# The 32-row block inversion of a gated delta rule, moved from VectorE to GpSimd

## The chip, the cores and the metric

The kernel runs on one core of a Trainium2 chip. A core has five engines that run beside each other, each through its own instructions in order: TensorE (PE; matmuls and transposes), VectorE (DVE; elementwise work and reductions), ScalarE (ACT; elementwise functions and copies), GpSimd (POOL; elementwise work and DMA issue) and SyncE (SP; here the main issuer of DMAs). They wait for each other through semaphores. The metric is the time of one execution in device microseconds (us).

## The reference: what is computed

A two-layer decoder trunk on 512 tokens of 1024 features. The first layer mixes tokens with a gated delta rule (6 heads of width 128), the second with a sliding-window attention; each layer also attends to 256 memory tokens and ends in a SwiGLU block. All weights are f32. What matters here is the triangular system that the delta rule solves for each head and chunk:

```python
decay = jnp.exp(jnp.where(tril, gc[..., :, None] - gc[..., None, :], -jnp.inf))
kb = k * beta[..., None]
lower = jnp.where(strict, jnp.einsum("bhncd,bhnkd->bhnck", kb, k) * decay, 0.0)
rhs = jnp.concatenate([v * beta[..., None], kb * jnp.exp(gc)[..., None]], axis=-1)
sol = lax.linalg.triangular_solve(lower, rhs, left_side=True, lower=True, unit_diagonal=True)
u, w = sol[..., :dv], sol[..., dv:]
...
def step(state, inp):
    u_n, w_n, a_n, qg_n, kg_n, gl_n = inp
    v_new = u_n - jnp.einsum("bhck,bhkv->bhcv", w_n, state)
    o_n = jnp.einsum("bhck,bhkv->bhcv", qg_n, state) + jnp.einsum("bhcs,bhsv->bhcv", a_n, v_new)
    state = state * gl_n[..., None, None] + jnp.einsum("bhck,bhcv->bhkv", kg_n, v_new)
    return state, o_n
```

## The kernel before

Activations lie transposed, features on partitions and the 512 tokens along the row. Each f32 product is made of three matmuls on parts of reduced precision: ScalarE rounds a weight tile of 128x1024 to `whi` (L138), VectorE subtracts it from the raw weight to get `wlo` (L151, called from `split`, L166), and TensorE multiplies (`mm3`, L196). A weight tile passes through three stations: a DMA on SP into `wraw` (two buffers), `whi` and `wlo` (three buffers each), and 24 matmuls of 512 columns into a PSUM bank `pj`.

The delta rule works on chunks of 128 tokens, 24 of them (6 heads by 4 chunks). For each the inverse of a unit lower triangular 128x128 matrix is needed. `gdn` (L552) writes the 32x32 blocks on its diagonals to DRAM (`basein`), and `base_inverse` (L772) reads all 96 of them back as one tile `big`, a block in each partition (L780). There the inversion runs in 31 steps of two elementwise operations (L786 to L791): step j multiplies what is left of column j of L by row j of X into `btmp`, and subtracts that from the rows of X below. Every operation needs the result of the one before it; the shapes go from 31x1 over 16x16 to 1x31, so at most 256 elements in a partition. Then ScalarE makes a transposed copy of X (`big<-big`, L793), two DMAs store X and the copy to DRAM (`basex`, `basext`, L797) and eight load them back as blocks of `X64` and `Tt` (L804, L809). `solve` (L812) builds the 64- and 128-row inverses from these with small matmuls on TensorE, and `scan_step` uses them.

Beside the inversion run the scores and the softmax against the memory tokens (`scores`, L909; `sm` are its rows, scaled by VectorE and ScalarE in `scale`, L987), their transposes on TensorE into two PSUM banks `g` (L148), ScalarE's copies of these to `pf` (L1028), and the projections of the queries with their convolution (`qv`, L542; the first tap on ScalarE, three on VectorE) and gating.

The order on each engine is not the order of the code: a scheduler lays the instructions out when the program is built, by its own estimates of durations, with `nosync` ties (L114) where the author wants an order. On the chip each engine then keeps to its order, and an instruction that waits holds up all that stand behind it on its engine.

Of the kernel before, what the change touches and what calls it, by code (L numbers as in the profile page):

```python
# [13 lines left out]
ALU = mybir.AluOpType  # L14
# [70 lines left out]
class Builder:  # L85
# [686 lines left out]
    def base_inverse(self, gp, base_in, after):  # L772

        nc = self.nc
        n = NH * NB
        e = BASE * BASE
        whole = self.t(gp, [P, 4 * T], F32, "big")
        big = lambda i: whole[:n, i * e:(i + 1) * e].rearrange("p (a b) -> p a b", b=BASE)
        L = big(0)
        nc.sync.dma_start(L.rearrange("p a b -> p (a b)"), base_in.rearrange("n b e -> (n b) e"))  # L780
        X = big(1)
        Xf = X.rearrange("p a b -> p (a b)")
        clear = lambda out, value: self.nosync(nc.vector.memset(out, value).ins, after)
        clear(Xf, 0.0)
        clear(Xf[:, ::BASE + 1], 1.0)
        for j in range(BASE - 1):  # L786
            r, w = BASE - 1 - j, j + 1
            tmp = self.t(gp, [n, 256], F32, "btmp", 2)[:, :r * w].rearrange("p (i m) -> p i m", m=w)
            self.tt(nc.vector, tmp, L[:, j, j + 1:].unsqueeze(2).to_broadcast([n, r, w]),
                    X[:, j, :w].unsqueeze(1).to_broadcast([n, r, w]), ALU.mult)  # L790
            self.tt(nc.vector, X[:, j + 1:, :w], X[:, j + 1:, :w], tmp, ALU.subtract)  # L791
        Xt = big(0)
        self.copy(Xt, X.rearrange("p i m -> p m i"))  # L793
        outs = []
        for nm, src in (("basex", X), ("basext", Xt)):
            d = self.t(self.dpool, [NH, NB, BASE * BASE], F32, nm)
            nc.sync.dma_start(d.rearrange("n b e -> (n b) e"), src.rearrange("p a b -> p (a b)"))  # L797
            outs.append(d)
        X64 = self.t(gp, [P, NH, 2 * BASE], F32, "X64")
        clear(X64, 0.0)  # L800
        for b in range(NB):
            s = slice(b * BASE, (b + 1) * BASE)
            o = b % 2 * BASE
            nc.sync.dma_start(X64[s, :, o:o + BASE], outs[0][:, b, :].rearrange("n (i m) -> i n m", m=BASE))  # L804
        Tt = self.t(gp, [P, NH, P], F32, "Tt")
        clear(Tt, 0.0)
        for b in range(NB):
            s = slice(b * BASE, (b + 1) * BASE)
            nc.sync.dma_start(Tt[s, :, s], outs[1][:, b, :].rearrange("n (m i) -> m n i", i=BASE))  # L809
        return X64, Tt  # L810
# [916 lines left out]
```

## Time and profile before

| | us |
|---|---|
| three runs | 1116.79, 1117.61, 1118.80 (median 1117.61) |
| profiled execution, whole | 1117.12 |
| its span (first to last instruction) | 1115.4 |
| the inversion on VectorE, first start to last end | 110.98 to 148.61 |
| first use of its result on TensorE | 174.85 |

The profile lists, for one execution, the busy time of each engine, the chain of work that ended last, groups of equal instructions, and on request a timeline. A timeline row gives the start, the duration, the engine, the line, the operation with out<-in, and in brackets how long the engine had been idle and what ended that. "SPq" is SyncE's DMA queue. Matmuls are pipelined, so the starts of neighbouring ones tell more than their durations. The mean clock granted to TensorE was 0.999 of full speed.

### The profile page before, as it was taken

The page shows a single profiled execution, that of the slowest core. Times are in us where ns is not written, and L with a number is a line of the kernel's source. Part 1 is how long each engine was busy: PE and PEld are TensorE (multiplying, and loading weights), DVE is VectorE, ACT ScalarE, POOL GpSimd, SP SyncE. Part 2 cuts the span into 40 slices and gives each one's busy share as a digit, 9 for nine tenths or more (in the row PEclk, how much of TensorE's full clock was granted, in tenths as well). Part 3 has the DMA queues.
Part 4 walks back from the last instruction along what each step waited for, and adds up shares of the span by engine and source line. Part 5 has one row for each costly group of instructions (what it writes and reads, how often), then busy time and mean ns, then how long its engine had stood idle before and what let it go on. Part 6 is the DMA issues. An engine that isn't in the chain of part 4 may idle for free.

```text
span 1115.4 us, 21263 instructions
## 1 busy us (share of the span) xinstructions
PE 1103.7 (99%) x7957; PEld 1000.7 (90%) x7957; DVE 937.2 (84%) x1878; ACT 695.0 (62%) x1462; POOL 105.9 (9%) x129
## 2 busy tenths in 40 slices
PE   9999999999999999999999999999999999999997
PEld 8888778877889999999998777788899999999996
DVE  7676976667899999999997877839999899998964
ACT  8588674456566656665565655856766566655644
POOL 0000000000011111111110000000121111111101
PEclk9999999999999999999999999999999999999999
DMA  8344352234577777777753321115677877787622
GB/s 318 107 149 146 107 135 87 86 104 133 153 165 193 188 194 187 180 198 180 198 138 99 125 68 40 54 58 150 152 188 182 199 188 181 190 193 190 153 85 90
DMA packets 81146, 165.36 MB, mean 148 GB/s; under 512 B 18588, under 2 KB 20148, under 8 KB 81044
## 3 DMA queue, kind: packets, MB, share of 16 engines
q1 hardware_dynamic: 64436, 133.87, 38.1%
q0 software_dynamic: 16320, 29.89, 16.5%
q8 instruction: 62, 1.02, 0.4%
q14 instruction: 40, 0.33, 0.1%
q10 hardware_dynamic: 288, 0.26, 0.1%
HBM read 156.98 MB, written 7.01 MB: 147 GB/s over the span
## 4 chain that ended last, share of the span: by engine, by line
PE 84%; DVE 12%; ACT 2%; issue 1%; DMA 1%; DVEq 0%; ACTq 0%; SPq 0%
PE g L144 49%; PE pj L144 23%; PE sc L144 6%; DVE wlo L151 3%; PE qk L144 3%; PE pt L144 1%; DVE fu L151 1%; PE pt L148 1%; DVE x L151 1%; DVE l L154 1%; DVE T L151 1%; PE g L148 1%; DVE sqa L151 1%; DMA wraw<-in_wgu 1%; ACT h L138 1%
## 5 line engine op out<-in xcount | busy, mean ns | idle before, releaser
L138 ACT ACTIVATE whi<-wraw 128x512 fp32r<-128x512 f32 (+2 forms) x357 | 251.5, 712 | 154.9 <-PE g L144 70.1
L151 DVE TENSOR_TENSOR wlo<-wraw,whi 128x512 fp32r<-128x512 f32 (+2 forms) x357 | 280.6, 792 | 34.7 <-ACT whi L138 29.6
L144 PE MATMUL g<-T,whi 128*128 128x256 f32 x1280 | 229.2, 280 | 1.0 <-ACT fs L138 0.6
L144 PE MATMUL g<-h,whi 128*128 128x256 f32 (+1 forms) x780 | 222.5, 286 | 1.7 <-ACT h L138 1.5
L144 PE MATMUL g<-l,whi 128*128 128x256 f32 (+1 forms) x780 | 222.4, 285 | 0.0
L144 PE MATMUL g<-h,wlo 128*128 128x256 f32 (+1 forms) x780 | 222.1, 285 | 0.0
L144 PEld LDWEIGHTS g<-T,whi 128*128 128x128 f32 x1280 | 194.9, 188 | 2.1 <-ACT fs L138 1.1
L144 PE MATMUL pj<-h,whi 128*128 128x512 f32 (+1 forms) x460 | 182.1, 399 | 0.0
L144 PE MATMUL pj<-l,whi 128*128 128x512 f32 (+1 forms) x460 | 180.2, 392 | 0.4 <-DVE l L154 0.3
L144 PE MATMUL pj<-h,wlo 128*128 128x512 f32 (+1 forms) x460 | 179.7, 391 | 0.0
L144 PE MATMUL g<-T,wlo 128*128 128x256 f32 x640 | 178.4, 279 | 0.0
L144 PEld LDWEIGHTS g<-h,whi 128*128 128x128 f32 x780 | 146.3, 188 | 4.3 <-ACT h L138 2.5
L144 PEld LDWEIGHTS g<-l,whi 128*128 128x128 f32 x780 | 146.6, 188 | 1.8
L144 PEld LDWEIGHTS g<-h,wlo 128*128 128x128 f32 x780 | 146.6, 188 | 1.7
L144 PEld LDWEIGHTS g<-T,wlo 128*128 128x128 f32 x640 | 120.3, 188 | 0.0
L144 PEld LDWEIGHTS pj<-h,whi 128*128 128x128 f32 x460 | 86.3, 188 | 20.8 <-issue 4.1
L144 PEld LDWEIGHTS pj<-h,wlo 128*128 128x128 f32 x460 | 86.5, 188 | 18.0 <-issue 0.9
L144 PEld LDWEIGHTS pj<-l,whi 128*128 128x128 f32 x460 | 86.6, 188 | 17.6 <-DVE l L154 1.2
L138 ACT ACTIVATE whi<-ws 128x512 fp32r<-128x512 f32 x112 | 70.3, 628 | 47.0 <-PE g L144 45.6
L151 DVE TENSOR_TENSOR wlo<-ws,whi 128x512 fp32r<-128x512 f32 x112 | 76.9, 687 | 3.7 <-ACT whi L138 3.7
L1374 POOL DMA_DIRECT2D ws<-in_wgu x40 | 35.1, 878 | 438.2 <-DVE l L154 203.8
L138 ACT ACTIVATE fs<-g 128x256 f32<-128x256 f32 x168 | 61.2, 367 | 1.3 <-PE g L144 0.9
(398 smaller groups left out, 1927.2 us busy)
## 6 DMA issues: line engine op xcount, KB each, us to landing
wraw<-in_wgu SPq DMA_DIRECT2D x48, 512.0 KB
ws<-in_wgu SPq DMA_DIRECT2D x80, 256.0 KB
ws<-in_wgu POOLq DMA_DIRECT2D x80, 256.0 KB, 4.9
wraw<-in_win SPq DMA_DIRECT2D x26, 512.0 KB
wraw<-in_wgu SPq DMA_DIRECT2D x40, 256.0 KB
wraw<-in_wout SPq DMA_DIRECT2D x16, 512.0 KB
ws<-in_wdn SPq DMA_DIRECT2D x32, 256.0 KB
ws<-in_wdn POOLq DMA_DIRECT2D x32, 256.0 KB, 5.1
```

The lines of the kernel that those rows point to most:

```text
L138: self.copied = self.nc.scalar.activation(out, in_, AF.Copy, **kw).ins
L144: return self.nc.tensor.matmul(out, lhsT, rhs, start=start, stop=stop, skip_group_check=more).ins
L148: return self.nc.tensor.transpose(out, in_, self.ident[:k, :k]).ins
L151: return eng.tensor_tensor(out=out, in0=a, in1=b, op=op).ins
L154: return self.nc.vector.scalar_tensor_tensor(out=out, in0=in0, scalar=scalar, in1=in1, op0=op0, op1=op1).ins
L1374: nc.gpsimd.dma_start(s1, a22, accum_op=ALU.add)
```

## The change

The engine of the two operations in each of the 31 steps:

```diff
         for j in range(BASE - 1):
             r, w = BASE - 1 - j, j + 1
             tmp = self.t(gp, [n, 256], F32, "btmp", 2)[:, :r * w].rearrange("p (i m) -> p i m", m=w)
-            self.tt(nc.vector, tmp, L[:, j, j + 1:].unsqueeze(2).to_broadcast([n, r, w]),
+            self.tt(nc.gpsimd, tmp, L[:, j, j + 1:].unsqueeze(2).to_broadcast([n, r, w]),
                     X[:, j, :w].unsqueeze(1).to_broadcast([n, r, w]), ALU.mult)
-            self.tt(nc.vector, X[:, j + 1:, :w], X[:, j + 1:, :w], tmp, ALU.subtract)
+            self.tt(nc.gpsimd, X[:, j + 1:, :w], X[:, j + 1:, :w], tmp, ALU.subtract)
```

All shapes and data stay the same. The 62 instructions leave VectorE's list and stand on GpSimd's between the last of four early DMA issues (L484) and a memset (L1485), with the library load (`ISA`) that GpSimd's elementwise operations need ahead of them; before, that load stood ahead of four such operations at the end of the program. The scheduler also lays out the other engines anew around this place.

On ScalarE, behind the softmax of the first two memory heads (`sm_1275`, `sm_1276` are its rows, `qm_248` the second memory query, `big_1344` X and its transposed copy, `whi_1603` and `whi_1698` the rounded weights of two query projections):

```order
-L138 ACTIVATE sm_1275<-sm_1275,den_1278 128x256
+L138 ACTIVATE sm_1275<-sm_1275,den_1278 128x256 x2
 L138 ACTIVATE qm_248_1310<-pj_1318 128x512
-L138 ACTIVATE sm_1275<-sm_1275,den_1278 128x256
 L138 ACTIVATE sm_1276<-sm_1276,den_1278 128x256 x2
+L138 ACTIVATE big_1344<-big_1344 96x1024
 L138 ACTIVATE whi_1603<-wraw_1601 128x1024
 L138 ACTIVATE whi_1698<-wraw_1696 128x1024
```

The transposed copy of X has moved ahead of `whi_1603`; before, it stood sixteen rows behind that, after `whi_1828`. Behind `whi_1698` follow, before and now, the first tap of `qv_1590` and four copies `pf` of transposes. Also, `whi_1729` has moved back by some ten rows, behind the exponentials of the second softmax.

On SP, the loads of the query weights (`wraw`), the stores of the squared queries (`q<-sq`), and the way of the inverse through DRAM:

```order
 L177 DMA wraw_1696<-in_win 128x1024
-L177 DMA wraw_1727<-in_win 128x1024
-L177 DMA wraw_1826<-in_win 128x1024
-L695 DMA q_314_1647<-sq_1645 128x512
-L177 DMA wraw_2096<-in_win 128x1024
-L695 DMA q_317_1659<-sq_1657 128x512
 L797 DMA basex_1442<-big_1344 96x1024
 L797 DMA basext_1444<-big_1344 96x1024
 L804 DMA X_288_1446<-basex_1442 32x24x32 x4
 L809 DMA Tt_1452<-basext_1444 32x24x32 x4
+L695 DMA q_314_1647<-sq_1645 128x512
+L177 DMA wraw_1727<-in_win 128x1024
```

The stores and loads of the inverse now stand ahead of three weight loads and two stores that they used to follow; `wraw_2096` comes six rows further down, behind the store of the third squared query (`q_337`).

On TensorE the order at this place is the same before and now: projections of the queries (`pj_1519`) with the transposes of the softmax (`g`) and the products with the memory values (`sc_1527`) in between:

```order
 L148 MATMUL g_1531<-consts_66,sm_1275 128x128 x4
 L148 MATMUL g_1539<-consts_66,sm_1275 128x128 x4
 L144 MATMUL pj_1519<-h_506,whi_1515 128x512
 L148 MATMUL g_1552<-consts_66,sm_1276 128x128 x4
 L144 MATMUL sc_1527<-pf_1528,m_64_414 64x256 x2
```

Nothing moved here; the rows are those on which TensorE depends on ScalarE's `pf` copies. Further differences on TensorE and VectorE are shifts of neighbouring rows by a few places later in the same stage.

## Prediction

> **What bounds the kernel now.** I read the page first: shares, the tenths by slice, the chain that ended last.
>
> ```profile
> PE 1103.7 (99%) x7957; PEld 1000.7 (90%) x7957; DVE 937.2 (84%) x1878; ACT 695.0 (62%) x1462; POOL 105.9 (9%) x129
> PE 84%; DVE 12%; ACT 2%; issue 1%; DMA 1%; DVEq 0%; ACTq 0%; SPq 0%
> ```
>
> TensorE is the bound of the whole program: it carries 84% of the chain and is hardly ever without a matmul. A change elsewhere can win only where TensorE waits, and loses wherever it makes TensorE wait. GpSimd has next to nothing to do. The second view is busy time by stretch, over the time in which the inversion runs (columns: length; busy time and count of PE, PEld, DVE, ACT, POOL; granted clock).
>
> ```profile
> 111.00:127.70 16.70, 16.70 (x81) 13.40 (x80) 15.68 (x46) 11.57 (x27) 0.00 (x0) 1.00 0.35 116
> 132.60:148.60 16.00, 15.54 (x87) 11.67 (x86) 15.60 (x38) 7.63 (x12) 0.00 (x0) 1.00 0.28 97
> ```
>
> VectorE is full here (15.68 of 16.70, 15.60 of 16.00), which is what makes the move look attractive. But TensorE stands still for only 0.46 us of the later 16 us and for none of the earlier. Freeing VectorE can therefore give back about 0.5 us, not the time that VectorE is freed of.
>
> The third view is the timeline of VectorE and ScalarE at the two ends of the inversion.
>
> ```profile
> 110.98 0.19 DVE L151 TENSOR_TENSOR btmp<-big 96x31 f32<-96x31 f32 x1 [1.95 <-DMA big<-basein]
> 111.20 0.21 DVE L151 TENSOR_TENSOR big<-big,btmp 96x31 f32<-96x31 f32 x1
> ...
> 127.69 0.42 DVE L151 TENSOR_TENSOR btmp<-big 96x256 f32<-96x256 f32 x1
> ...
> 148.43 0.18 DVE L151 TENSOR_TENSOR big<-big,btmp 96x31 f32<-96x31 f32 x1
> ```
>
> ```profile
> 126.52 1.30 ACT L138 ACTIVATE sm<-sm,den 128x256 f32<-128x256 f32 x3
> 127.72 1.05 ACT L138 ACTIVATE whi<-wraw 128x1024 fp32r<-128x1024 f32 x1
> 129.95 1.06 ACT L138 ACTIVATE whi<-wraw 128x1024 fp32r<-128x1024 f32 x1 [1.18 <-PE pj L144]
> 130.91 0.67 ACT L138 ACTIVATE qv<-pj,gains 128x512 f32<-128x512 f32 x1
> 131.98 1.09 ACT L138 ACTIVATE pf<-g 128x512 f32<-128x512 f32 x2 [0.40 <-PE g L148]
> ...
> 148.70 2.00 ACT L138 ACTIVATE big<-big 96x1024 f32<-96x1024 f32 x1 [0.36 <-DVE big L151]
> 150.61 0.63 ACT L132 ACTIVATE qv<-qv 128x512 f32<-128x512 f32 x1
> ```
>
> The inversion starts when its input lands (110.98) and ends at 148.61. ScalarE's transposing copy of X (`big<-big`, L793) follows 0.09 us later and waited only 0.36 us, because it stands late in ScalarE's order. Its result is needed only by the solve's matmuls:
>
> ```profile
> 174.85 1.71 PE L144 MATMUL sc<-X,N 32*32 32x32 f32 x96
> ```
>
> So by the data there are 26 us of slack, and an inversion on a slower engine would be harmless **if nothing else stood behind it**. That is the question on which the forecast turns, and the instruction order answers it: in the changed program the copy stands ahead of `whi_1603`, right behind the scalings of `sm` that end at 127.82, where it used to stand sixteen rows later. ScalarE takes its instructions in order, so from 127.8 on it does nothing until GpSimd has finished.
>
> **The change, term by term.** Removed from VectorE: 62 operations (the window table, for the tile `btmp` alone).
>
> ```profile
> 111.00:148.70 37.70, 20.80 (x62) 1.00 0.31 105
> ```
>
> That is 20.80 us of work. Added to GpSimd: the same 62, with 2 x 5,456 = 10,912 elements in each partition (the sum of (31-j)(j+1) over j). Before has only four operations of this kind on GpSimd, and a few memsets:
>
> ```profile
> L151 POOL TENSOR_TENSOR T<-T,ws 128x256 f32<-128x256 f32 x4 | 2.8, 730 | 56.8 <-ACT ws L132 56.8
> L1485 POOL MEMSET sinT<- 128x512 f32 x1 | 0.5, 525 | 180.5 <-PE sc L144 180.5
> L283 POOL MEMSET ones<- 128x128 f32 x1 | 0.2, 204 | 0.3 <-POOLq L1718 0.3
> L1718 POOL MEMSET const-float32-0.0<- 128x1 f32 x1 | 0.1, 98 | 0.2 <-issue 0.2
> ```
>
> For 256 elements GpSimd takes 730 ns where VectorE takes 420 (127.69), a factor of 1.74. **Value taken:** 20.80 x 1.74 = 36.2 us. Bounds come from how the 730 ns divide. If the fixed part is only that of the smallest memset (98 ns), an element costs 2.47 ns and the 62 cost 6.1 + 26.9 = 33.0 us. If an element costs no more than in a memset ((525-204)/384 = 0.84 ns), the fixed part is 516 ns and they cost 32.0 + 9.1 = 41.1 us.
>
> Each of the 62 reads what the one before it wrote, so each also pays a hand-over. VectorE's is 0.03 us (110.98 + 0.19 to 111.20). The nearest row on GpSimd is its start behind ScalarE:
>
> ```profile
> 1104.01 0.38 ACT L132 ACTIVATE ws<-g 128x256 f32<-128x256 f32 x1
> ...
> 1104.47 1.43 POOL L151 TENSOR_TENSOR T<-T,ws 128x256 f32<-128x256 f32 x2 [53.65 <-ACT ws L132]
> ```
>
> It is 0.08 us, so 62 x 0.08 = 5.0 us; I take that, with 1.9 us (VectorE's gap) and 9.9 us (twice the row) as ends. The same row shows that the library load, an instruction that stood just ahead of this pair, cost nothing visible behind a long idle time. In the changed program it stands ahead of the inversion, where GpSimd has been idle since its last DMA issue (39.8 us), so it is taken at nothing.
>
> ```profile
> 38.69 1.07 POOL L484 DMA_DIRECT2D mk<-kt  x2 [4.34 <-DVE kt L151]
> ```
>
>
> GpSimd thus ends at 111.0 + 36.2 + 5.0 = **152.2 us**, with ends 145.9 and 162.0.
>
> What stands behind it: the copy starts at 152.2 + 0.09, `whi_1603` 1.91 later (148.70 to 150.61), then `whi_1698` and the `qv` scaling at 0.96 each (129.95 to 130.91) and, about 0.6 later, the first `pf` copy: 152.2 + 4.5 = 156.7, where it used to start at 131.98. The two waits of 1.18 and 0.40 in these rows are absorbed in that. **Delay 24.7 us**; in general the end of GpSimd's work minus 127.5.
>
> TensorE has nothing with which to cover it:
>
> ```profile
> 131.34 1.03 PE L148 MATMUL g<-consts,sm 128*128 128x128 f32 x8
> 132.13 0.47 PE L144 MATMUL pj<-h,whi 128*128 128x512 f32 x1
> 132.63 0.66 PE L148 MATMUL g<-consts,sm 128*128 128x128 f32 x4
> ```
>
> It makes eight transposes into the two `g` banks and one matmul; the next four transposes (132.63) need a `g` bank that only the `pf` copy frees, and every later matmul stands behind them. So TensorE stands still from about 132.4 to 157, and the delay goes through in full, since it is the bound from here to the end.
>
> **What is late next.** (a) After the pause TensorE may run slowly at first, as at the start of the program:
>
> ```profile
> 1.19 3.57 PE L144 MATMUL g<-wabs 128*128 128x256 f32 x15 [1.19 <-DVE eps L292]
> ...
> 6.62 0.29 PE L144 MATMUL pj<-mh,whi 128*128 128x256 f32 x1
> 6.74 0.28 PE L144 MATMUL pj<-ml,whi 128*128 128x256 f32 x1
> ```
>
> Fifteen matmuls of 256 columns took 0.24 us each there, and 0.12 from 6.62 on: some 5.4 us at half rate, 2.7 us lost. The granted clock of the page reads full throughout, so it doesn't decide what this was. I take 2 us, with ends 0 and 2.7. The Trainium skill ("TensorE: Matmul & The Clock Gate", section "What's actually happening") says that an idle window of about 3.4 us halves TensorE's clock until it has been busy for about as long. By that rule alone some 3.4 us at half rate would cost 1.7 us; without it the sum would be 2 us less.
>
> (b) On SP the two stores and eight loads of the inverse (148.63 to 156.38 in before) now stand ahead of three weight loads, and SP waits for GpSimd in front of them. The first two of those weights are wanted some 20 us after ScalarE resumes, and take cover behind `pj_1607` and `pj_1702`. The third, `wraw_2096`, now is issued behind the square of the third query, about 14 us later than before relative to TensorE's work:
>
> ```profile
> 143.05 0.33 SPq L177 DMA_DIRECT2D wraw<-in_win  x1
> ...
> 148.63 0.33 SPq L797 DMA_DIRECT2D basex<-big  x1
> ...
> 154.10 2.28 SPq L809 DMA_DIRECT2D Tt<-basext  x4
> ...
> ws<-in_wgu POOLq DMA_DIRECT2D x80, 256.0 KB, 4.9
> ```
>
> At 4.9 us or more for a landing (half its size took that), it comes about 2 us after ScalarE wants it, with two `pf` copies behind. I take 1 us, ends 0 and 3. (c) VectorE's freed time gives back the 0.5 us named above.
>
> Sum against the profiled execution (1117.12 us, 0.5 under the median of the runs shown): 24.7 + 2 + 1 - 0.5 = 27.2, so **1144.3 us**. Least: 145.9 - 127.5 - 0.5 = 17.9, or 1135. Most: 162.0 - 127.5 + 2.7 + 3 = 40.2, or 1157, and 1161 with the first rival.
>
> **The rivals.** *GpSimd and VectorE hinder each other.* Nothing in before shows it: GpSimd's four operations hardly differ (723 to 737 ns), and what VectorE ran beside them (`T<-T,g`) has one of its inputs in PSUM. VectorE still has two weight splits and four scalings before ScalarE stops:
>
> ```profile
> 114.03 1.21 DVE L151 TENSOR_TENSOR wlo<-wraw,whi 128x1024 fp32r<-128x1024 f32 x1
> ...
> 117.96 1.23 DVE L151 TENSOR_TENSOR wlo<-wraw,whi 128x1024 fp32r<-128x1024 f32 x1 [0.15 <-ACT whi L138]
> ...
> 124.74 0.34 DVE L994 TENSOR_SCALAR sm<-sm,den 128x256 f32<-128x256 f32 x1
> ...
> L151 POOL TENSOR_TENSOR T<-T,ws x4: 723/729/737, 1104.5 to 1109.7; 128x256 f32<-128x256 f32 x4
> ```
>
> If GpSimd stands still for all six it ends 3.8 us later: 1148. If VectorE's few operations wait instead, nothing changes. Chance 0.3, within the range. The Trainium skill ("SBUF — State Buffer", section "Who interferes with whom") has this as a lock on a shared port pair, held for a whole instruction; no run so far shows it.
>
> *The rows are too short for GpSimd.* The four known operations have rows of 128; the inversion's have 1 to 31, 992 rows in all. If a row costs as much again as its elements (36.2 / 992 = 0.036 us each), the inversion ends at 188 and the program at 1180. For it speaks nothing, against it nothing either. Chance 0.07.
>
> *Not slower: the wait never binds.* If GpSimd were done by 127.8, ScalarE's copy would find X ready. That needs 16.8 us for 62 operations, 0.27 us each, against 0.73 for the only size known; decisive point 0.27 us. Then the 0.5 us of TensorE's waits are won and the 2 us copy sits in idle time: 1116.6, no measurable change. The same if ScalarE could pass the copy by, which an in-order engine can't. A true gain would need more waiting on TensorE than the windows show. Chance 0.05, and 0.02 for a gain beyond 0.2%, about the least that a measurement of this kernel can tell from no change.
>
> **How the numbers follow.** Forecast (ScalarE blocked behind GpSimd, with or without the first rival): 0.86; short rows 0.07; not slower 0.07. The range 1132 to 1162 takes in the ends of the unknown costs and both forms of the forecast, and leaves out the short rows and the no-change case. Chances: faster 0.02, same 0.05, slower 0.93.
>
> **What would show it.** GpSimd's 62 operations should take 33 to 45 us from about 111, with 0.7 us for 256 elements and gaps under 0.16. ScalarE should show one wait of about 24 us in front of `big<-big`, released by GpSimd; TensorE a hole from about 132 to 157 that ends with a `pf` copy; behind it the same rows as before, shifted. Matmuls right behind the hole should be at half rate for a few us. I am wrong if ScalarE's wait is short, if GpSimd's operations take under 0.3 us, or if the rows at 175 stand where they stood.

## Result and the profile after

| | us |
|---|---|
| before, median of 4 runs beside the changed kernel | 1118.07 (1116.79 to 1118.80) |
| changed, median of 4 runs | 1143.63 (1141.50 to 1144.40) |
| ratio | 1.0227, 95% interval 1.0215 to 1.0239 |
| profiled execution of the changed kernel, whole / span | 1143.81 / 1142.0 |

The change costs 25.6 us. The page of the changed kernel, first part and two rows of the slices:

```profile
PE 1107.3 (97%) x7957; PEld 1003.6 (88%) x7957; DVE 921.3 (81%) x1816; ACT 695.4 (61%) x1462; POOL 138.5 (12%) x191
...
PE   9999659999999999999999999999999999999997
...
PEclk9999869999999999999999999999999999999999
```

TensorE does the same 7957 matmuls in about the same busy time (1107.3 us, 1103.7 before). Its share falls from 99% to 97% because of one hole, the 6 and the 5 in the fifth and sixth of 40 slices. The granted clock falls at the same place. VectorE is 15.9 us less busy (937.2 to 921.3), and that shows nowhere in the time.

The hole in the windows (columns: length; busy time and count of PE, PEld, DVE, ACT, POOL; granted clock), and the inversion alone on GpSimd (window table for the tile `btmp`):

```profile
132.60:157.00 24.40, 2.49 (x13) 1.53 (x13) 3.84 (x5) 5.37 (x6) 15.20 (x31) 0.58 0.22 49
155.10:160.10 5.00, 4.99 (x19) 3.33 (x20) 2.51 (x4) 1.93 (x4) 0.00 (x0) 0.50 0.84 133
```

```profile
111.50:150.20 38.70, 33.78 (x62) 0.82 0.15 50
```

Until GpSimd ends at 150.15, every other engine stands idle in the hole: the work of ScalarE (5.37 us) and VectorE (3.84 of 24.40 us) comes behind that. The timelines of ScalarE and TensorE name the waits:

```profile
127.91 0.90 ACT L138 ACTIVATE sm<-sm,den 128x256 f32<-128x256 f32 x2
150.18 1.94 ACT L138 ACTIVATE big<-big 96x1024 f32<-96x1024 f32 x1 [21.38 <-POOL big L151]
152.02 1.99 ACT L138 ACTIVATE whi<-wraw 128x1024 fp32r<-128x1024 f32 x2
153.91 0.67 ACT L138 ACTIVATE qv<-pj,gains 128x512 f32<-128x512 f32 x1
154.48 1.07 ACT L138 ACTIVATE pf<-g 128x512 f32<-128x512 f32 x2
```

```profile
132.73 0.47 PE L144 MATMUL pj<-h,whi 128*128 128x512 f32 x1
155.11 1.11 PE L148 MATMUL g<-consts,sm 128*128 128x128 f32 x4 [21.91 <-ACT pf L138]
156.16 1.98 PE L144 MATMUL sc<-pf,m 128*64 128x256 f32 x8
```

GpSimd's last subtraction ends at 150.15. ScalarE has waited 21.38 us for it with the copy of X, and TensorE 21.91 us for the `pf` copy that stands four instructions behind that copy. The eight products `sc<-pf,m` behind the hole take 1.98 us where they took 1.08.

How the loss builds up is read from equal rows of TensorE in both kernels, before first, then after:

```profile
136.75 0.50 PE L144 MATMUL pj<-h,wlo 128*128 128x512 f32 x1
150.88 0.59 PE L144 MATMUL sc<-m,qm 64*128 64x256 f32 x2
158.36 1.06 PE L144 MATMUL g<-qv,kn 128*128 128x128 f32 x8
```

```profile
161.59 0.50 PE L144 MATMUL pj<-h,wlo 128*128 128x512 f32 x1
174.66 0.59 PE L144 MATMUL sc<-m,qm 64*128 64x256 f32 x2
183.97 1.05 PE L144 MATMUL g<-qv,kn 128*128 128x128 f32 x8
200.48 1.71 PE L144 MATMUL sc<-X,N 32*32 32x32 f32 x96
```

The last matmul ahead of the hole already stands 0.60 us later than before (132.13 to 132.73). This is no work of the change: equal matmuls at 21 us, long before the inversion, are already 0.57 us apart. From there the shift grows to 22.48 at the transposes behind the hole (132.63 to 155.11), to 24.84 at 161.59, falls to 23.78 at 174.66, rises to 25.61 at 183.97 and is 25.63 at 200.48. So the terms are +21.88 (the wait), +2.36 (slow rows), -1.06 (small waits of before that are gone), +1.83 (a second place, at about 182). The sum is 25.0 us. The spans of the two executions differ by 26.6 us (1142.0 and 1115.4): besides these 25.0 and the 0.60 from the start, about 1.0 us more arises later than 200 us, most of it between 500 and 610 us, in work that the change doesn't touch. Its cause stays open.

### The profile page after: what moved, and what is told of

It is laid out like the page before. It is cut to its first block, busy times and chain, and to the rows that moved or that the text cites. A ratio compares the mean times of both kernels' runs of the same rounds, so it can differ in the third digit from the quotient of the medians.

```text
span 1142.0 us, 21267 instructions
## 1 busy us (share of the span) xinstructions
PE 1107.3 (97%) x7957; PEld 1003.6 (88%) x7957; DVE 921.3 (81%) x1816; ACT 695.4 (61%) x1462; POOL 138.5 (12%) x191
## 4 chain that ended last, share of the span: by engine, by line
PE 80%; DVE 9%; ACT 3%; POOL 3%; issue 2%; DMA 1%; SPq 0%; DVEq 0%; ACTq 0%; POOLq 0%
PE g L144 47%; PE pj L144 22%; PE sc L144 6%; DVE wlo L151 3%; PE qk L144 3%; POOL big L151 2%; POOL btmp L151 1%; PE pt L144 1%; DVE fu L151 1%; PE pt L148 1%; PE g L148 1%; ACT whi L138 1%; DVE x L151 1%; DVE T L151 1%; DVE l L154 1%
```

## Experiments

Two theories stood against each other. **Wait**: GpSimd's time costs nothing by itself, and what costs is that engines which take their work in order stand behind it. **Hindrance**: GpSimd's operations slow what runs beside them, or cost in some other way, whoever waits.

### The copy of X later (late_blocks, late_blocks_dve)

The function is cut in two, so that copy, stores and loads come after the next three query projections: the copy is tied behind ScalarE's work for the second memory head, the stores behind the load of the first value weight. The inversion stays where it was; late_blocks_dve is the same with the inversion on VectorE.

```diff
+            if h0:
+                first_v = self.load(a["win"][2 * H])
+                X, every_t = self.base_blocks(gp, *inverse, self.weighed_at, self.loaded)
...
-        Xt = big(0)
+        return X, big(0), clear
+
+    def base_blocks(self, gp, X, Xt, clear, copied, loaded):
...
         self.copy(Xt, X.rearrange("p i m -> p m i"))
+        self.nosync(self.copied, copied)
...
-            nc.sync.dma_start(d.rearrange("n b e -> (n b) e"), src.rearrange("p a b -> p (a b)"))
+            self.nosync(nc.sync.dma_start(d.rearrange("n b e -> (n b) e"), src.rearrange("p a b -> p (a b)")).ins, loaded)
```

> The inversion stays on GpSimd; ScalarE's transposing copy of X now stands behind mq1h (166 us in the trace of before), and SyncE's stores and loads of the inverse behind the load of the first value weight. Theory 'wait' (the 26.5 us are ScalarE standing in its order behind GpSimd, and TensorE behind ScalarE): no engine waits for GpSimd, so 1117 to 1119 us, as before the change, with TensorE's idle time before the transposes of sm under 1 us where it was 21.9. Theory 'hindrance' (GpSimd's operations slow VectorE and others beside them, whoever waits): 62 operations still run beside a busy VectorE, so at least a quarter of the loss stays: 1124 us or more. GpSimd's chain should get longer under both, since now VectorE works beside it: 38.6 us plus about 1.1 for each wlo that it meets.

> The same new places of the copy, the stores and the loads, with the 62 operations back on VectorE: the control for late_blocks. Theory 'wait': the places cost nothing, 1116 to 1119 us; and as the prediction gives the 20.8 us freed on VectorE only 0.5 us, late_blocks and this one lie within 1.5 us of each other. Rival ('VectorE binds here too'): the freed 20.8 us are worth more, and late_blocks is faster than this one by 2 us or more. Theory 'hindrance': this one is faster than late_blocks by 6 us or more.

Measured: late_blocks 1122.19 us, 1.0034 (1.0022 to 1.0046) of before; late_blocks_dve 1118.02 us, 1.0001 (0.9992 to 1.0010). Of 25.6 us some 4 stay, which is neither what wait said nor the 6 us that hindrance said. SyncE's queue, ScalarE and TensorE in late_blocks show where they go:

```profile
155.13 0.33 SPq L807 DMA_DIRECT2D basex<-big  x1
155.51 0.42 SPq L695 DMA_DIRECT2D q<-sq  x1
```

```profile
159.15 0.63 ACT L693 ACTIVATE sq<-qv 128x512 f32<-128x512 f32 x1 [3.24 <-DMA q<-sq]
```

```profile
163.47 1.73 PE L148 MATMUL g<-consts,sm 128*128 128x128 f32 x8 [3.13 <-DVE DT L151]
```

The store of X itself (`basex`) came out of the scheduler ahead of the store of a squared query. SyncE waited with it for GpSimd, the squared query lay behind it, and ScalarE waited 3.24 us for that query's only buffer. TensorE waited 3.13 us in turn, behind work of VectorE that depends on ScalarE, and the granted clock was 0.50 from 163.7 to 167.1. On SyncE, then, the same thing happens as on ScalarE.

### Both stores later too (late_stores, late_stores_dve)

```diff
-            nc.sync.dma_start(q2[h], sq)
+            self.q_stored = nc.sync.dma_start(q2[h], sq).ins
...
-                X, every_t = self.base_blocks(gp, *inverse, self.weighed_at, self.loaded)
+                X, every_t = self.base_blocks(gp, *inverse, self.weighed_at, self.q_stored)
```

> As late_blocks, with both stores of the inverse tied behind the store of the third squared query. In late_blocks the first of them (basex) stood on SyncE from 143 to 155 us for GpSimd, the store of a squared query behind it, and ScalarE's next square behind that for 3.24 us (its only buffer). Theory 'wait' (the 4.2 us of late_blocks are this third list that waits in order): 1117 to 1119 us, TensorE's busy time between 160 and 200 us back from 36.5 to over 39 us, and no wait of ScalarE for q. Theory 'hindrance' (GpSimd's operations cost it): 1121 us or more, as in late_blocks.

> The same places, with the inversion on VectorE: the control for late_stores. Theory 'wait' with the prediction's 0.5 us for a freed VectorE: within 1.5 us of late_stores. If VectorE's 20.8 us bind here: slower than late_stores by 2 us or more. If hindrance: faster than late_stores by 3 us or more.

Measured: late_stores 1118.12 us, 1.0003 (0.9994 to 1.0012); late_stores_dve 1118.57 us, 1.0010 (1.0001 to 1.0018). Against late_blocks, both stores of the inverse are now tied behind the store of the third squared query. A window of late_stores, then of late_stores_dve:

```profile
130.00:160.00 30.00, 29.98 (x163) 23.70 (x163) 20.74 (x36) 20.19 (x42) 20.41 (x33) 1.00 0.33 110
```

```profile
130.00:160.00 30.00, 29.55 (x157) 23.11 (x156) 26.72 (x63) 18.98 (x40) 0.00 (x0) 1.00 0.32 110
```

With all 62 operations still on GpSimd, beside a VectorE that works, nothing is lost: hindrance as a cause of the 25 us falls. GpSimd's chain even takes longer here (110.75 to 152.92, 42.2 us and not 38.6), since it meets more work of VectorE, and that costs nothing either. What the freed VectorE is worth shows only in TensorE's busy time, 29.98 of 30 us and not 29.55. The medians differ by 0.45 us the same way, but their intervals overlap, so a gain in time is not shown. The version on GpSimd without the waits is thus as fast as the kernel before; none of the versions tried beat it.

### The copy on GpSimd (copy_pool)

```diff
-        self.copy(Xt, X.rearrange("p i m -> p m i"))
+        nc.gpsimd.tensor_copy(Xt, X.rearrange("p i m -> p m i"))
```

> The transposing copy of X is done by GpSimd itself, behind its 62 operations; ScalarE's list loses this one instruction and keeps its order there, and SyncE's stores and loads of the inverse stay ahead of the weight loads that they passed. GpSimd ends at about 150.2 plus 2 to 3 us for the copy. Theory 'ScalarE is the one that holds TensorE': the 21.9 us before the transposes and the 2.4 us of slow clock behind them go; what stays is SyncE's list: wraw_1727 is issued at about 153 and not 139, its parts are ready at about 159 where TensorE needs them at 156, and two more weights follow behind eight loads: 3 to 8 us, so 1121 to 1126 us. Rival 'SyncE holds nothing that is needed': 1117 to 1119. Rival 'hindrance, or GpSimd is waited for elsewhere too': over 1130.

Measured: 1136.95 us, 1.0178 (1.0163 to 1.0192), far from the 1121 to 1126 expected and in the range of the last rival, of which the second half is true: GpSimd is waited for elsewhere too. SyncE, ScalarE and TensorE in this kernel:

```profile
154.22 0.38 SPq L177 DMA_DIRECT2D wraw<-in_win  x1
```

```profile
159.94 1.06 ACT L138 ACTIVATE whi<-wraw 128x1024 fp32r<-128x1024 f32 x1 [22.46 <-DMA wraw<-in_win]
```

```profile
165.25 2.08 PE L144 MATMUL g<-qv,kn 128*128 128x128 f32 x8 [18.92 <-ACT qv L132]
```

The wait of 21.9 us at the transposes is gone, as expected, but ScalarE stands for 22.46 us all the same. The load of `wraw_1727` is issued only behind the inverse's stores (`basext` at 153.80), and the scheduler, which does not know that, placed its rounding ahead of the next `qv`. I had reckoned with a late weight, not with what was queued behind it on ScalarE. With this order on ScalarE, SyncE's list costs 19.0 us without the copy of X: taking one engine out of the wait hands it to the next.

### The wait without GpSimd (early_dve)

The kernel before, inversion on VectorE, with one tie that puts ScalarE's copy of X ahead of a weight:

```diff
+            w = self.weight(a["win"][h0 + 2], after=() if h0 else (self.turned_x,))
+            ps += (self.project(None, self.h, w=w),)
...
+        self.turned_x = self.copied
```

> The kernel before, inversion on VectorE, with one tie: ScalarE rounds the third query weight behind the copy of X (it comes out behind the pf copies and the second qv). Nothing runs on GpSimd here that did not before. Theory 'wait': VectorE ends the inversion at about 148.6, ScalarE's copy takes 2.0 and the rounding 1.0, so the weight is there at about 151.7 where TensorE needs it at about 140: some 11 us, with 2.4 us of slow clock behind them and up to 2 us of later weights: 1128 to 1133 us with no work on GpSimd at all. Rival 'the loss needs GpSimd': 1117 to 1119 us.

Measured: 1128.22 us, 1.0093 (1.0079 to 1.0107), with nothing new on GpSimd. TensorE in this kernel:

```profile
146.42 0.50 PE L144 MATMUL pj<-h,whi 128*128 128x512 f32 x1 [4.42 <-ACT whi L138]
...
178.45 0.79 PE L144 MATMUL pj<-h,wlo 128*128 128x512 f32 x1 [1.62 <-DVE wlo L151]
```

The time is right, its parts are not: VectorE ended already at about 143.4, so the wait is 4.42 us and not 11; the rest is a wait of 0.86 us earlier, one of 1.62 us later, and two stretches at a lower clock, 0.50 from 146.9 to 150.4 and the second in this window:

```profile
177.66:184.48 6.82, 6.03 (x14) 4.77 (x15) 6.39 (x9) 2.21 (x3) 0.00 (x0) 0.50 0.47 124
```

That an order alone can make a loss of this kind is shown.

### More work on GpSimd, with and without the wait (double_mul, late_double)

In both, each multiplication is done twice. In double_mul a tie (that of early_dve) keeps the copy early on ScalarE; late_double is late_stores otherwise.

```diff
-            self.tt(nc.gpsimd, tmp, ...
+            for _ in range(2):
+                self.tt(nc.gpsimd, tmp, ...
```

> Each of the 31 multiplications is done twice (the second gives the same result), and the rounding of the third query weight is tied behind the copy of X so that the copy stays early on ScalarE; it comes out behind the first two pf copies instead of ahead of them. 31 multiplications more at 0.48 us (from the rows of the changed kernel, 15.0 us without the stretched one) and 0.077 us between two: GpSimd's chain 17.4 us longer, its end at about 167.6. Theory 'wait': the time follows GpSimd's end one to one, less what ScalarE now has done already (about 2): 1157 to 1161 us. Rival 'only a part of the loss is the wait, the rest a fixed price of the new order': well under one to one, 1150 us or less.

> late_stores with each of the 31 multiplications done twice. In late_stores GpSimd ended at 152.9 and the first instructions that need the result stood ready at 156.2 (SyncE, basex) and 165.5 us (ScalarE, the copy), TensorE's sc<-X,N at 173.9. 17.4 us more put GpSimd's end at about 170.3. Theory 'wait' (the operations cost nothing until the first list reaches a row that needs them, and then what is past the cover): stores, loads and copy come about 5 us later for ScalarE and X lands at about 176 to 178 where TensorE asks at 173.9; 2 to 6 us with the slow clock, 1120 to 1124 us. Rival 'GpSimd's time costs by itself': 1135 us, as 17 us more cost in double_mul. Rival 'still covered': 1118.

Measured: double_mul 1161.28 us, 1.0390 (1.0377 to 1.0404); late_double 1128.16 us, 1.0102 (1.0087 to 1.0117). ScalarE and TensorE in double_mul, then in late_double:

```profile
167.15 1.94 ACT L138 ACTIVATE big<-big 96x1024 f32<-96x1024 f32 x1 [33.06 <-POOL big L151]
```

```profile
170.10 1.97 PE L144 MATMUL sc<-pf,m 128*64 128x256 f32 x8 [33.67 <-ACT pf L138]
...
181.73 1.95 PE L144 MATMUL g<-qv,kn 128*128 128x128 f32 x16
196.81 0.80 PE L144 MATMUL pj<-h,whi 128*128 128x512 f32 x1 [4.26 <-ACT whi L138]
```

```profile
172.68 1.94 ACT L138 ACTIVATE big<-big 96x1024 f32<-96x1024 f32 x1 [7.40 <-POOL big L151]
```

```profile
179.81 2.08 PE L144 MATMUL g<-qv,kn 128*128 128x128 f32 x8 [7.03 <-ACT qv L132]
```

In double_mul GpSimd ends 17.0 us later than in the changed kernel (167.12 for 150.15), and the program takes 17.65 us more, just above the 1157 to 1161 expected. The totals agree one to one, the path does not. ScalarE got two `pf` copies and a `qv` done ahead of its wait, so TensorE's wait grew by 11.8 us only (33.67 for 21.91). A further 5.1 us were lost at a second place: from the sixteen products `g<-qv,kn` to the next ones (200.70) TensorE takes 18.97 us, and 13.85 in the changed kernel, because it waits 4.26 us for a weight that ScalarE rounds behind the second softmax, with a clock of 0.50 from 196.1 to 202.9. That the totals meet is luck; shown is that the wait grows when GpSimd ends later.

In late_double, GpSimd's end moved by 19.7 us (152.92 to 172.65) and the program by 10.0 (11 by the ratios to the kernel before, which ran beside each of the two). The first 12.6 us (from 152.9 to the copy at 165.47 in late_stores) were covered; past that ScalarE waits 7.40 and TensorE 7.03 us, with slow clock behind (0.50 from 179.8 to 189.4). The 2 to 6 us expected were too few: GpSimd ended 2.4 us later than reckoned, TensorE stood not for X but for a `qv` behind the copy, and the slow clock lasted longer.

### The slow rows behind the hole (warm, warm98)

Unused matmuls fill TensorE's wait:

```diff
+            if not own and m == 0 and n == 1:
+                hh = self.h[0][0]
+                for _ in range(90):
+                    ins = self.mm(o, hh[:, :P], hh)
+                    self.nosync(ins, turned)
+                    turned = ins
+                self.ahead = turned
```

> The changed kernel with 90 matmuls of 128x512 more, whose results nothing uses, on TensorE in the 22 us in which it waits (90 x 0.227 = 20.4 us). Theory 'the slow rows behind the wait come from the pause': the eight sc<-pf,m then take 1.08 us and not 1.98, and 2.4 us go: 1141 to 1141.8 us. Rival 'they come from something else that is late there (the copies, the loads)': the rows stay as long, 1143 to 1145 us.

> As warm, with 98 of the unused matmuls in place of 90. In warm the 90 ended at 152.9 and TensorE still waited 1.96 us; then the clock was 1.0 until about 155.6, 0.5 until about 158.4, and 1.0 again. 98 x 0.230 = 22.5 us end at 154.8, so no pause stays. Theory 'even a pause of 2 us brings the slow clock': the clock stays at 1.0, the eight sc<-pf,m take 1.08 us, and about 1.4 us (half of 2.8) go: 1139.3 to 1140.2 us. Rival 'the slow clock comes from something else at this place': 0.5 again for some us, 1141 us as in warm.

Measured: warm 1141.05 us, 1.0210 (1.0194 to 1.0226); warm98 1141.60 us, 1.0215 (1.0198 to 1.0232). TensorE in warm with windows behind its wait (columns: length, busy time and count of PE, granted clock, DMA share, GB/s), then in warm98:

```profile
154.88 1.50 PE L144 MATMUL sc<-pf,m 128*64 128x256 f32 x8 [1.96 <-ACT pf L138]
```

```profile
154.88:155.40 0.52, 0.52 (x6) 1.00 1.14 178
155.90:158.40 2.50, 2.50 (x13) 0.50 1.03 162
```

```profile
155.09 1.08 PE L144 MATMUL sc<-pf,m 128*64 128x256 f32 x8 [0.70 <-ACT pf L138]
...
159.58 1.08 PE L144 MATMUL sc<-pf,m 128*64 128x256 f32 x8 [1.46 <-ACT pf L138]
```

On the rows the theory holds. In warm98, with no long wait left, the clock is 1.00 from 153 to 160 and the products take 1.08 us. In warm a wait of 1.96 us was left, and the clock was 0.50 for 3.4 us (155.4 to 158.8). On the time the theory does not hold: warm98 is no faster than warm. At full clock TensorE waits for ScalarE instead (0.70 and 1.46 us), since the scheduler here placed a `qv` that waits for VectorE ahead of the second pair of `pf` copies. So the pause is shown to be the cause of the slow clock, while what the slow clock alone costs this program stays open: 2.36 us by the rows, less where ScalarE would have been late anyway. What warm gains in time may come from elsewhere: in its order `whi_1729` stands early again, which led to the next run.

### The second place (whi_first, after_again)

The changed kernel with the exponentials tied behind the rounding of `whi_1729`, and the changed kernel once more beside it:

```diff
-            steps = self.projected(a["win"][first + 1], self.h)
+            w = self.weight(a["win"][first + 1])
+            if m:
+                for e in self.exps:
+                    self.nosync(e, self.copied)
+            steps = self.projected(None, self.h, w=w)
...
+                        self.exps.append(self.fn(
```

> The changed kernel with the eight exponentials of the second softmax tied behind the rounding whi_1729, so that this weight stands on ScalarE where the kernel before had it, ahead of them. In the changed kernel it came at 180.46 and TensorE waited 0.67 us for it at 181.60 and 0.61 us for its wlo at 182.94; by its rows 1.83 us were lost there. Theory 'whi_1729 behind the exponentials is the last term': both waits gone, 1.2 to 1.9 us less than the changed kernel run beside it. Rival 'the softmax comes later in turn and TensorE waits for that': within 0.6 us of it.

> The changed kernel itself, on the same chip beside whi_first, as the measure for it: 1143 to 1144.5 us where the kernel before takes 1117 to 1118.5.

Measured: whi_first 1138.95 us, 1.0202 (1.0188 to 1.0216); after_again 1142.36 us, 1.0225 (1.0212 to 1.0239). TensorE in the changed kernel, then in whi_first:

```profile
170.12 1.95 PE L144 MATMUL g<-qv,kn 128*128 128x128 f32 x16
...
181.60 0.50 PE L144 MATMUL pj<-h,whi 128*128 128x512 f32 x1 [0.67 <-ACT whi L138]
182.94 0.50 PE L144 MATMUL pj<-h,wlo 128*128 128x512 f32 x1 [0.61 <-DVE wlo L151]
```

```profile
168.84 1.95 PE L144 MATMUL g<-qv,kn 128*128 128x128 f32 x16
180.82 1.06 PE L144 MATMUL g<-qv,kn 128*128 128x128 f32 x8
```

Both waits are gone. From the sixteen to the next eight products `g<-qv,kn` whi_first takes 11.98 us, the changed kernel 13.85 (170.12 to 183.97, shown above): 1.87 less, the term of 1.83. The medians differ by 3.4 us, more than the 1.2 to 1.9 expected of the tie. Some 1.1 us of the rest arose ahead of this place: GpSimd's chain ended 0.63 us earlier (149.15 for 149.78 in after_again), and the clock of 0.50 behind the hole lasted 4.5 us and not 5.5. The tie explains neither, and what is left stays open. after_again itself came out 0.6 us under the 1143 expected.

## Why the prediction was right, and where its sizes were off

The forecast was 1144.3 us, slower with a chance of 0.93; measured 1143.63. Point by point:

- **TensorE bounds; VectorE's freed time is worth 0.5 us.** Right as far as it can be seen: late_stores against its control has 0.43 us more of TensorE's busy time in the window; in the time of the program the difference is not clear of noise.
- **The copy of X blocks ScalarE from 127.8 until GpSimd is done, and TensorE behind it.** Right, row by row (21.38 and 21.91 us). Shown from three sides: the loss goes when nothing stands behind the result (late_stores), grows when GpSimd ends later and something does (double_mul), and some of it comes without GpSimd when only the order is like this (early_dve).
- **GpSimd's end at 152.2, delay 24.7.** Mis-sized: 41.2 us were forecast from start to end, 38.57 measured. The hand-overs were right (5.0 forecast; 38.57 - 33.78 = 4.79 measured). The operations were put at 36.2 us, as 1.74 times VectorE's; they took 33.78. Without what VectorE added to two of them (next point) they took 31.6, under my lower end of 33.0. Both took 256 elements to cost 730 ns, as in `T<-T,ws`; with 255, a subtraction takes 676 and a multiplication 626. Nor is the factor over VectorE a constant: a multiplication of 31 elements takes 232 ns where VectorE takes 190, a factor of 1.2. The groups of GpSimd by shape in the changed kernel:

```profile
L151 POOL TENSOR_TENSOR big<-big,btmp 96x256 f32<-96x256 f32 x1 | 0.7, 729 | 0.1
L151 POOL TENSOR_TENSOR big<-big,btmp 96x255 f32<-96x255 f32 x2 | 1.4, 676 | 0.2
L151 POOL TENSOR_TENSOR btmp<-big 96x255 f32<-96x255 f32 x2 | 1.3, 626 | 0.2
L151 POOL TENSOR_TENSOR big<-big,btmp 96x31 f32<-96x31 f32 x2 | 0.5, 259 | 0.2
L151 POOL TENSOR_TENSOR btmp<-big 96x31 f32<-96x31 f32 x2 | 0.5, 232 | 71.3 <-DMA big<-basein 71.2
```

  From 31 to 255 elements a subtraction costs (676 - 259) / 224 = 1.86 ns an element and 0.20 us fixed, a multiplication 1.76 ns and 0.18 us; with the 5,456 elements and 31 operations of each kind that is 31.5 us. (The subtraction of 256 elements, 729 ns, lies above this line.) Why the multiplications are cheaper is not shown: they differ from `T<-T,ws` in the operation, in the shapes and in having both inputs broadcast. The delay formula (end less 127.5) was right: with the shift of 0.60 us taken off, 149.55 - 127.5 = 22.1 against 21.9. The length of the rows hardly matters: a subtraction of 31 rows of one element takes 0.27 us, one of a single row of 31 takes 0.25, which is under 1 ns a row where the rival of short rows had 36. It is out.
- **Rival, GpSimd and VectorE hinder each other, up to 3.8 us.** It happened, at 2.2 us. Beside VectorE's two weight splits (1.23 us each, from 113.83 and from 118.56) these two operations of GpSimd were stretched:

```profile
113.83 1.46 POOL L151 TENSOR_TENSOR btmp<-big 96x112 f32<-96x112 f32 x1
118.58 1.59 POOL L151 TENSOR_TENSOR big<-big,btmp 96x175 f32<-96x175 f32 x1
```

  Their twins of the same shape took 0.37 and 0.51 us (from the means of the pairs, 914 and 1052 ns), so they lost 1.09 and 1.08. The four scalings of `sm` did not hold GpSimd up by such an amount; there VectorE lost, which cost nothing, as the rival's other half said.
- **(a) Slow clock, 2 us.** 2.36 by the rows, granted clock 0.50 for 5 us behind the hole. The pause as its cause is shown by warm98; its price in the program is not.
- **(b) SyncE's list, 1 us, at `wraw_2096`.** This step failed: `wraw_2096` cost nothing (the shift is 25.61 at 183.97 and 25.63 at 200.48). The 1.83 us came from the first of the two weights that "take cover". Its load was issued at about 161.5, but its rounding had moved behind the exponentials on ScalarE, to 180.46. I had seen that move in the order and given it no price. Shown by whi_first.
- **(c) -0.5 us.** -1.06 in the shifts, between 136.75 and 150.88 of the kernel before.

The delay was 2.8 us too long. The smaller terms came to 3.1 us where 2.5 were forecast, and 1.6 us of the profiled execution's difference (0.60 ahead of the place, about 1.0 far behind it) had no term at all. That these nearly cancel, and that (b), priced for the wrong weight, came near what another one cost, is luck; the wait of 21.9 us, which is most of the loss, is not.

## What to carry to other kernels

Before moving work to an idle, slower engine, look for what consumes its last result, on which engine and which DMA queue, and how many instructions stand behind that consumer in order; by the data there were 26 us of slack here, and the order left none of it. Moving one consumer is not enough: the copy, both stores and a weight load behind them each made a wait of their own. A bottleneck is not relieved by unloading an engine that is only busy: with all waits gone, 20.8 us off VectorE brought no gain clear of noise.

## What the runs showed of the hardware that was not expected

**VectorE and GpSimd stop each other, operation by operation, and either side can lose.** In the changed kernel GpSimd's operation lost 1.1 us beside each of two `wlo`. VectorE's four scalings of `sm` show the other side; the changed kernel, and the later four in late_stores, when GpSimd was done:

```profile
125.57 2.96 DVE L994 TENSOR_SCALAR sm<-sm,den 128x256 f32<-128x256 f32 x4
```

```profile
155.51 1.14 DVE L1004 TENSOR_SCALAR sm<-sm,den 128x256 f32<-128x256 f32 x4
```

In late_stores, operations of GpSimd were stretched beside each `wlo` that ran during the inversion (a subtraction of 255 elements took 1.55 us at 129.41, 0.68 at 134.18) and beside `gcr<-gcr,qv`; both read two tiles of SBUF. They were not stretched beside `qv<-pj,gains,qv`, whose `pj` lies in PSUM. VectorE lost there too: three of the `wlo` took 1.34 to 1.67 us and not 1.23. The Trainium skill ("SBUF — State Buffer", section "Who interferes with whom") states that a VectorE instruction with two SBUF inputs contends with a GpSimd instruction that reads SBUF, one in a two-port mode contends with GpSimd as well, and that whoever comes second there is blocked for the whole instruction. The trace agrees, at 1.1 us for a `wlo` of 1.23.

**A short pause can be enough for the slow clock.** In warm, TensorE had been at full clock and waited 1.96 us; about 0.5 us after it resumed the clock fell to 0.50, for 3.4 us. In early_dve it fell within a wait of 1.62 us (176.8 to 178.45), for 6.8 us. In warm98, waits of 0.70 and 1.46 us left it at 1.00. In the long holes it fell 3.2 us after their start in the changed kernel and 5.3 us after it in whi_first. So the length of a pause alone does not decide it. The Trainium skill ("TensorE: Matmul & The Clock Gate", section "What's actually happening") gives windows of about 3.4 us, free-running: an idle one brings the slow clock, a busy one ends it. That the moment varies fits this, and so does the length of the slow stretch in warm; behind the hole of the changed kernel it was 5.1 us, and 9.6 us behind the wait in late_double. The pause that brings it was shorter here than such a window, and the measurement decides.
